# Stepping a state-space layer through the forget-gate attention, with score corrections over 128 rows and neighbourhood keys by column

## The chip, the cores and the metric

The kernel runs on 1 core of one Trainium2 chip. The metric is the device time of the whole program in microseconds; the time before is the median of 3 runs.

## The reference

The input is one sequence of 512 tokens (an 8 x 64 grid) with 1024 features. Two layers of a first block are followed by one layer of a second block, all in float32.

```python
# first block, twice: three branches, gated and merged
y_a = neighbourhood_attention(na_q, na_k, na_v, na_rpb)  # 8 heads of 64; 8 rows x 16 columns of keys
y_b = gqa_attention(q, k, gq_v)                          # 8 query heads, 2 key heads
y_c = spatial_gating(sg_u, sg_v, ...)
merged = sum(sigmoid(gate_r) * ((y_r * silu(z_r)) @ w_br_r) for r in "abc")
h = layer_norm(ALPHA * x + merged @ w_out + b_out)
...
# second block: forget-gate attention, a chunked state-space mixer, a diagonal state-space layer
s = q @ k.T / 8 + cum[q] - cum[k]                        # causal, cum = cumsum(log_sigmoid(f))
y_fox = softmax(s) @ v                                   # 8 heads of 64
y_ssd = ssd_mixer(z, xbc, dt_raw, ...)                   # conv, chunks of 128, 8 heads
y_s5 = glu(gelu(state_space(u)))                         # 32 groups of 16, complex state of 64
merged = sum(sigmoid(gate_r) * (y_r @ w_branch_r) for r in range(3))
x = layer_norm_2(ALPHA * x + merged @ w_out)
x = layer_norm_2(ALPHA * x + conv_ffn(x))
```

## The kernel before

Every product with weights keeps float32 accuracy by splitting each operand into a rounded high part and a low rest (`load_w`, L76 and L78, for weights) and adding three matmuls: high by high, low by high, high by low (`mm3`, L99 to L101). Low parts of weights are made on GpSimd or VectorE; `self.lo_gp` is a pattern of 0 (VectorE) and 1 (GpSimd) that is gone through load by load. Weight loads, and all other transfers, are issued on SP's queue.

Projections are *jobs*: one of 512 columns by 128 features is 24 matmuls in four portions of six. Jobs stand in `self.queue`; `fill(n)` runs n portions, so that the attention loops can put them between their own steps. The kernel is written with a tile framework: at build time a planner fixes the order of each engine's instructions from its own estimates of durations, with the written order as the priority, and adds the waits. So an instruction can stand before one that was written ahead of it, and a real duration that differs from the planner's shows up as a wait.

**Scores.** `heads_q` makes, for each head of a pair, a tile that holds the scaled query's high part on the head's 64 partitions and its low part on the other 64. `heads_k` makes a tile with the key's high part on both halves (L326, L327), and one tile `lo` for both heads, with each head's low part on that head's own 64 partitions (L328). A score is a matmul over 128 rows (q high and low against k high) and a correction over the head's 64 rows (q high against k low): L659 and L662 in `na`, L941 and L942 in `fox`. In `fox` a mask matmul in bf16 follows (L943).

**`na`** (neighbourhood attention, once in each layer of the first block) has 16 steps, four pairs of heads by four blocks of 16 columns. Keys lie in token order (row by row of the grid), so that a block's 256 keys are 8 pieces of 32; values are fetched from DRAM in the same order (L628), and the bias table goes with it (L634, L647).

**Second block.** `fox` queues its projections in a list `js` and then runs 34 iterations over 32 scores (8 heads by 4 query tiles); each calls `fill(1)` and `step(1)` twice. `ssd` does the same 16 times for `step`. `s5` is a generator that goes through the diagonal state-space layer in four groups F = 0 to 3: two matmul sets into two PSUM banks (L1408), rotations on VectorE and GpSimd (L1411 to L1417), two scans (L1422), rotations back (L1425 to L1431), the output matmuls (L1438, L1440), a GELU, a round trip through DRAM, and `close` (L1393, L1394). `step(n)` adds n to a counter and advances `s5` by one `yield` for each whole unit: `RF` per call in `fox`, `RS` in `ssd`, `RM` per portion in the first two merges. With `RF = 0.0` `s5` starts in `ssd`; a group needs the input `ub[F]`, which the job `uj(F)` projects and which passes through DRAM (`s5_in`, L1355 to L1360). PSUM has 3 banks for jobs ("mm"), 2 for scores ("s"), 2 for transposes ("t"), 1 for values ("v"); `s5` uses "mm" until the end of `ssd`, then "s" and "t".

Of the kernel before, what the change touches and what calls it, by code (L numbers as in the profile page):

```python
# [19 lines left out]
P = 128  # L20
# [5 lines left out]
class Net:  # L26
# [292 lines left out]

    def heads_k(self, src):  # L320

        nc, out, lo = self.nc, [], self.b2(F32R)
        for s in range(2):
            r, o = slice(64 * s, 64 * s + 64), slice(64 - 64 * s, 128 - 64 * s)
            k = self.b2(F32R)
            nc.scalar.copy(k[r], src[r])  # L326
            nc.scalar.copy(k[o], src[r])  # L327
            nc.vector.tensor_tensor(lo[r], src[r], k[r].bitcast(F32), op=ALU.subtract)  # L328
            out.append(k)
        return out, lo  # L330

    def z_gate(self, bias_name, bi, out):

# [256 lines left out]
    def na(self, l, vd):  # L590
# [12 lines left out]
        def kj(hp):  # L603
            def use(ps):
                kf = self.tmp()
                nc.scalar.activation(kf, ps, AF.Identity, bias=self.col(f"b{l}", 4 + hp))
                kzs[hp] = self.heads_k(kf)
            return self.fm_job(fm[4 + hp], use)

# [12 lines left out]

        def load(hp):
            vw = [self.b2(shape=(P, 4, P)) for _ in range(2)]
            vr = vd.rearrange("(r c) f -> r c f", c=64)
            for j in range(4):
                for half in range(2):
                    nc.sync.dma_start(vw[j // 2][:, 2 * (j % 2) + half], vr[4 * half:4 * half + 4, LO[j]:LO[j] + 32, hp * P:hp * P + P])  # L628
            vws[hp] = vw
            bts[hp] = []  # L630
            for s in range(2):
                t = self.ld(shape=(P, 8, 48))
                nc.sync.dma_start(t, a[f"rpb{l}"][2 * hp + s])
                bts[hp].append(t)  # L634

        def bias(i):

            if i == len(steps):
                return
            hp, j = steps[i]  # L640
            if j == 2:
                bms[i] = bms[i - 1]
                return
            bms[i] = self.b2(shape=(P, 2, 8, 32))
            x0 = (16, 8, 8, 0)[j]
            for s in range(2):
                nc.gpsimd.tensor_tensor(bms[i][:, s], bts[hp][s][:, :, x0:x0 + 32],  # L647
                                        self.namask[:, (0, 1, 1, 2)[j], None].to_broadcast([P, 8, 32]), op=ALU.add)

        def weights(hp, j):  # L650
            bm = bms[4 * hp + j]
            e = self.b2(shape=(P, 2, 256))
            mx, nmx, sm, rc = self.small(2), self.small(2), self.small(2), self.small(2)
            jq = slice(j * P, j * P + P)
            q, (ks, kl) = [x[:, jq] for x in qs[hp]], kzs[hp]
            ks, (kl,) = ([x.rearrange("p (r c) -> p r c", c=64)[:, :, LO[j]:LO[j] + 32] for x in xs] for xs in (ks, (kl,)))
            pss = [self.psum("s", (P, 256)) for _ in range(2)]
            for s in range(2):
                nc.tensor.matmul(pss[s], q[s], ks[s], start=True, stop=False)  # L659
            for s in range(2):  # L660
                r = slice(64 * s, 64 * s + 64)
                nc.tensor.matmul(pss[s], q[s][r], kl[r], start=False, stop=True)  # L662
            for s in range(2):
                nc.vector.tensor_tensor_reduce(out=e[:, s], in0=pss[s], in1=bm[:, s].rearrange("p r c -> p (r c)"), op0=ALU.add, op1=ALU.max,
                                               scale=1.0, scalar=-3e38, accum_out=mx[:, s:s + 1])
            nc.vector.tensor_scalar(nmx, mx, -1.0, None, op0=ALU.mult)
            for s in range(2):
                nc.scalar.activation(e[:, s], e[:, s], AF.Exp, bias=nmx[:, s:s + 1], accum_out=sm[:, s:s + 1])
            nc.vector.reciprocal(rc, sm)
            for s in range(2):  # L670
                nc.vector.tensor_scalar(e[:, s], e[:, s], rc[:, s:s + 1], None, op0=ALU.mult)
            return e
# [201 lines left out]
    def fox(self, xb, zz, step):  # L874
# [14 lines left out]
        def qj(hp):  # L889
            def use(ps):  # L890
                q[hp] = self.heads_q(ps, 0.125)
            return self.fm_job(fm[hp], use)
# [12 lines left out]
                xb[i] = z  # L905
            return self.fm_job(fm[12 + i], use)
        js = [self.tm_job([a[f"w2tm{c}"][0, 0], a[f"w2tm{c}"][0, 1]], vv(c)) for c in (1, 0)] + [qj(0), kj(0)]
        js += [xj(0), xj(1), qj(1), kj(1), xj(2), xj(3), qj(2), kj(2), xj(4), qj(3), kj(3), xj(5)]
        def zj(i):
            def use(ps):  # L910
                z = zz[i] = self.b2()
# [1 line left out]
                nc.scalar.activation(t, ps, AF.Tanh, scale=0.5)  # L913
                nc.vector.scalar_tensor_tensor(z, t, 1.0, ps, op0=ALU.add, op1=ALU.mult)
            return self.fm_job(fm[8 + i], use)
        js += [zj(i) for i in range(4)]

        def uj(F):
            return self.fm_job(fm[18 + F], lambda ps: self.s5_in(F, ps))
        self.ub = {}  # L920
        js += [uj(F) for F in range(4)]
        self.queue.append(self.jobs(js))
        self.fill(12)
        self.fdt(fd)
        self.lo_gp = (1, 1, 1, 0)
        self.fill(8)
        steps = [(hp, t, s) for hp in range(4) for t in range(4) for s in range(2)]
        sc, pes, cks, ys, po = {}, {}, {}, [], None
# [1 line left out]
        def weights(hp, t, s):  # L930
            h, n = 2 * hp + s, (t + 1) * P
            nn = max(n, 256)
            if t == 0:
                pc = self.psum("s")
                self.bcast_row(pc, h)
                cks[h] = self.b2()
                nc.scalar.copy(cks[h], pc)
            ps = self.psum("s")
            r = slice(64 * s, 64 * s + 64)
            qt, (ks, kl) = q[hp][s][:, t * P:t * P + P], kz[hp]  # L940
            nc.tensor.matmul(ps[:, :nn], qt, ks[s][:, :nn], start=True, stop=False)  # L941
            nc.tensor.matmul(ps[:, :nn], qt[r], kl[r, :nn], start=False, stop=False)  # L942
            nc.tensor.matmul(ps[:, n - P:n], self.identb, self.causal, start=False, stop=True)  # L943

            e = self.b2()
            mx, nm, sm, r = (self.small(1) for _ in range(4))
            nc.vector.tensor_tensor_reduce(out=e[:, :n], in0=ps[:, :n], in1=cks[h][:, :n], op0=ALU.subtract, op1=ALU.max,
                                           scale=1.0, scalar=-3e38, accum_out=mx)
            cq = self.cc[:, t, h:h + 1]
            nc.vector.tensor_scalar(nm, mx, cq, -1.0, op0=ALU.add, op1=ALU.mult)  # L950
            nc.vector.tensor_tensor(nm, nm, cq, op=ALU.add)
            nc.scalar.activation(e[:, :n], e[:, :n], AF.Exp, bias=nm, accum_out=sm)
            nc.vector.reciprocal(r, sm)
            return e, r
# [408 lines left out]
    def s5(self, gys, tags):  # L1363
# [34 lines left out]
        for F in range(4):  # L1398
# [33 lines left out]
            if F < 3:  # L1432
                w, tb = load(F + 1)
            yield
            py = self.psum(tags[1])
            for i in range(4):
                q = slice(i * P, i * P + P)
# [41 lines left out]
    def block2(self):  # L1479
# [1 line left out]
        gys = []  # L1481
        tags = ["mm", "mm"]
        s5 = self.s5(gys, tags)
        due = [0.0]

        def step(n):
            due[0] += n
# [10 lines left out]
        ya = self.fox(xb, zz, lambda n: step(RF))  # L1498
        yb = self.ssd(xb, zz, lambda n: step(RS))
        tags[:] = "s", "t"  # L1500
        self.lo_gp = (1,)
        merge(0, ya, RM, first=True)
        merge(1, yb, RM)
        for _ in s5:
# [43 lines left out]
NR = 6  # L1548
PSB = {"mm": 3, "s": 2, "t": 2, "v": 1}

RF = 0.0
RS = 0.5
RM = 1.5
BT = 4
MAGIC = 12582912.0
PI = 3.1415925
# [62 lines left out]
def _rpb_index():  # L1619
    r, cc = np.arange(P) // 16, np.arange(P) % 16  # L1620
    kr, x = np.arange(8), np.arange(48)
    ro = kr[None, :, None] - r[:, None, None] + 7
    co = np.clip(x[None, None, :] - 16 - cc[:, None, None] + 15, 0, 30)
    return (ro * 31 + co).reshape(-1)


def prepare(i):
# [18 lines left out]
    for l in range(2):  # L1646
        w, b = i["w_in"][l], i["b_in"][l]
        fmc = [w[:, 0:1024], w[:, 1536:2048], w[:, 2816:3328][:, pairs], w[:, 3328:3840], w[:, 4352:4864], w[:, 4864:7936]]
        a[f"w1fm{l}"] = _fm(np.concatenate(fmc, 1))
        tmc = [w[:, 2560:2816], w[:, 2048:2560], w[:, 3840:4352], w[:, 1024:1536]]  # L1650
        a[f"w1tm{l}"] = _tm(np.concatenate(tmc, 1))
        addc(f"b{l}", b.reshape(62, P).T)
        addc(f"zb{l}", b[2816:3328][pairs].reshape(4, P).T)
        addc(f"gvb{l}", b[2688:2816].reshape(P, 1))
        addr(f"qkb{l}", b[2048:2688])
        addr(f"qng{l}", np.concatenate([i["q_norm_g"][l], i["k_norm_g"][l]]))
        addr(f"sg{l}", np.concatenate([b[3840:4352], i["sg_ln_g"][l], i["sg_ln_b"][l]]))
        addr(f"b_out{l}", i["b_out"][l])
        addr(f"lnp_g{l}", i["ln_post_g"][l])
        addr(f"lnp_b{l}", i["ln_post_b"][l])  # L1660
        a[f"sgw{l}"] = np.ascontiguousarray(i["sg_w"][l].transpose(2, 0, 1))
        a[f"sgb{l}"] = np.ascontiguousarray(i["sg_b"][l].reshape(4, 2, P).transpose(1, 0, 2))
        a[f"rpb{l}"] = np.ascontiguousarray(i["na_rpb"][l].reshape(8, 15 * 31)[:, idx]).reshape(8, P, 8, 48)
        a[f"wbr{l}"] = np.stack([_pair(x) for x in (i["w_br_a"][l], i["w_br_b"][l][pairs], i["w_br_c"][l])])
        a[f"wout{l}"] = _wide(i["w_out"][l])
    w = i["w_in_2"][0]
# [59 lines left out]
```

## Time and profile before

| | |
|---|---|
| median of 3 runs | 2041.87 us (2039.82 to 2045.49) |
| profiled execution | 2042.89 us, its span 2041.1 us |
| TensorE busy (page) | 1988.1 us, 97% |
| VectorE, ScalarE, GpSimd busy | 1236.0 us, 863.2 us, 509.8 us |
| mean granted TensorE clock | 0.991 |

The span is the stretch that the profile covers; the time of the same execution is 1.8 us longer. A busy TensorE is one that has a matmul under way by the profile; the clock is the share of full speed that the chip granted.

### The profile page before, as it was taken

How to read it: one execution, taken by the hardware profiler on the slowest of the kernel's cores; microseconds unless marked ns; L12 is line 12 of the kernel's file. 1: busy time of each engine (PE TensorE's matmuls, PEld its weight loads, DVE VectorE, ACT ScalarE, POOL GpSimd, SP SyncE). 2: the span in 40 equal slices, each digit the busy share in tenths (PEclk: the TensorE clock that was granted, in tenths of full speed). 3: DMA queues.
4: the chain of work that ended last, by engine and by line, in shares of the span. 5: the costliest groups of instructions: out<-in, count | busy, mean ns of one | idle time of the engine just before them, and what ended most of it. 6: DMA issues, size and time to landing. Idle time of an engine off the chain costs nothing. (4 is left out here: it accounts for less than half of the span.)

```text
span 2041.1 us, 29326 instructions
## 1 busy us (share of the span) xinstructions
PE 1988.1 (97%) x10594; PEld 1653.3 (81%) x10594; DVE 1236.0 (61%) x2406; ACT 863.2 (42%) x1738; POOL 509.8 (25%) x594
## 2 busy tenths in 40 slices
PE   7999999999999999999999999998899999999998
PEld 7898877788799988777878877877688888888888
DVE  7776655766477766567545644365425477635655
ACT  3445446433235554564332466542233334423431
POOL 3343321100633436323610222235440000000000
PEclk9999999999999999999999999999899999999999
DMA  6432223333352322334353412143433423333332
GB/s 207 153 106 67 80 89 105 109 93 122 117 167 89 105 75 78 124 109 140 107 159 115 140 63 62 62 131 105 138 98 108 130 83 100 102 93 99 98 86 70
DMA packets 140464, 218.54 MB, mean 107 GB/s; under 512 B 19232, under 2 KB 44576, under 8 KB 140320
## 3 DMA queue, kind: packets, MB, share of 16 engines
q1 hardware_dynamic: 140320, 216.68, 33.7%
q8 instruction: 83, 1.36, 0.3%
q14 instruction: 61, 0.50, 0.1%
HBM read 196.70 MB, written 19.92 MB: 106 GB/s over the span
## 5 line engine op out<-in xcount | busy, mean ns | idle before, releaser
L76 ACT CAST wh<-wr 128x512 fp32r<-128x512 f32 x605 | 362.1, 618 | 587.5 <-PE psmm L100 273.7
L99 PE MATMUL psmm<-xh,wh 128*128 128x512 f32 (+1 forms) x1504 | 604.3, 402 | 1.5 <-DVE b L373 1.4
L100 PE MATMUL psmm<-xl,wh 128*128 128x512 f32 (+1 forms) x1504 | 588.1, 391 | 0.3 <-DVE xl L262 0.3
L101 PE MATMUL psmm<-xh,wl 128*128 128x512 f32 (+1 forms) x1504 | 587.4, 391 | 0.2 <-DVE wl L78 0.2
L78 DVE TENSOR_TENSOR wl<-wr,wh 128x512 fp32r<-128x512 f32 x526 | 374.6, 723 | 348.9 <-ACT wh L76 341.4
L101 PEld LDWEIGHTS psmm<-xh,wl 128*128 128x128 f32 x1504 | 283.5, 189 | 61.6 <-DVE wl L78 1.8
L99 PEld LDWEIGHTS psmm<-xh,wh 128*128 128x128 f32 x1504 | 284.1, 189 | 60.8 <-issue 3.4
L100 PEld LDWEIGHTS psmm<-xl,wh 128*128 128x128 f32 x1504 | 284.4, 189 | 52.7 <-DVE xl L262 0.7
L247 POOL TENSOR_TENSOR sm<-sm,mhalf 128x1 f32<-128x1 f32 x20 | 18.9, 947 | 648.4 <-DVE sm L245 648.4
L78 POOL TENSOR_TENSOR wl<-wr,wh 128x512 fp32r<-128x512 f32 x79 | 109.7, 1401 | 229.2 <-ACT wh L76 228.7
L99 PE MATMUL psmm<-wh,xh 128*128 128x256 f32 (+1 forms) x512 | 148.3, 291 | 2.0 <-DVE b L373 1.3
L100 PE MATMUL psmm<-wl,xh 128*128 128x256 f32 (+1 forms) x512 | 147.1, 287 | 2.0 <-DVE wl L78 1.8
L101 PE MATMUL psmm<-wh,xl 128*128 128x256 f32 (+1 forms) x512 | 147.3, 288 | 0.4 <-DVE xl L262 0.4
L465 POOL TENSOR_SCALAR b<-b,sm 128x512 f32<-128x512 f32 x64 | 101.1, 1580 | 163.6 <-DVE sm L296 158.4
L99 PE MATMUL psmm<-b,wh 128*128 128x512 f32 x304 | 119.8, 394 | 0.0
L100 PE MATMUL psmm<-b,wh 128*128 128x512 f32 x304 | 118.6, 390 | 0.0
L101 PE MATMUL psmm<-b,wl 128*128 128x512 f32 x304 | 118.5, 390 | 0.0
L99 PEld LDWEIGHTS psmm<-wh,xh 128*128 128x128 f32 x512 | 99.4, 195 | 4.0 <-DVE b L373 1.7
L100 PEld LDWEIGHTS psmm<-wl,xh 128*128 128x128 f32 x512 | 99.5, 194 | 3.8 <-DVE wl L78 2.6
L101 PEld LDWEIGHTS psmm<-wh,xl 128*128 128x128 f32 x512 | 99.4, 194 | 0.9 <-DVE xl L262 0.9
L647 POOL TENSOR_TENSOR b<-ld,namask 128x256 f32<-128x256 f32 x48 | 42.7, 916 | 151.0 <-PE psv L699 57.3
L294 ACT ACTIVATE b<-pss,sm 128x512 f32<-128x512 f32 x64 | 44.1, 689 | 81.5 <-DVE sm L291 81.0
(393 smaller groups left out, 3304.3 us busy)
## 6 DMA issues: line engine op xcount, KB each, us to landing
wr<-in_w1fm SPq DMA_DIRECT2D x192, 256.0 KB
wr<-in_w2fm SPq DMA_DIRECT2D x92, 256.0 KB
wr<-in_wup SPq DMA_DIRECT2D x88, 256.0 KB
wr<-in_wbr SPq DMA_DIRECT2D x72, 256.0 KB
wr<-in_w1tm SPq DMA_DIRECT2D x56, 256.0 KB
wr<-in_wout SPq DMA_DIRECT2D x48, 256.0 KB
wr<-in_wdown SPq DMA_DIRECT2D x43, 256.0 KB
ld<-in_rows SPq DMA_DIRECT2D x32, 256.0 KB
```

The costliest lines, as they stand in the source:

```text
L76: nc.scalar.copy(hi[:, c], raw)
L78: eng.tensor_tensor(lo[:, c], raw, hi[:, c].bitcast(F32), op=ALU.subtract)
L99: mm(ps, wh, xh, start=(first and k == 0), stop=False)
L100: mm(ps, wh, xl, start=False, stop=False)
L101: mm(ps, wl, xh, start=False, stop=(last and k == n - 1))
L247: nc.gpsimd.tensor_tensor(rs, ve, self.mhalf[:, :1], op=ALU.pow)
L294: nc.scalar.activation(e[:, :n], src, AF.Exp, bias=nm, scale=scale, accum_out=sm)
L465: nc.gpsimd.tensor_scalar(e, e, r, None, op0=ALU.mult)
L647: nc.gpsimd.tensor_tensor(bms[i][:, s], bts[hp][s][:, :, x0:x0 + 32], self.namask[:, (0, 1, 1, 2)[j], None].to_broadcast([P, 8, 32]), op=A ...
```

## The change

`heads_k` makes a tile `lo` for each head and copies the key's low part to the other 64 partitions too, so that the correction becomes a matmul over 128 rows. In `na` keys, values, bias table and mask are ordered column by column, which makes a block's keys one piece of 256. In `fox` the list of jobs is reordered: `uj` comes early, and most of `xj` late. `s5` gets one more `yield` ahead of the output matmuls, its counter starts at -7, `RF` becomes 0.5 and `RM` 0.5. The pattern of `lo_gp` becomes (0, 1) from `fox` to the end of the second merge.

```diff
     def heads_k(self, src):
-        nc, out, lo = self.nc, [], self.b2(F32R)
+        nc, out = self.nc, []
         for s in range(2):
...
-            k = self.b2(F32R)
+            k, lo = self.b2(F32R), self.b2(F32R)
             nc.scalar.copy(k[r], src[r])
             nc.scalar.copy(k[o], src[r])
             nc.vector.tensor_tensor(lo[r], src[r], k[r].bitcast(F32), op=ALU.subtract)
-            out.append(k)
-        return out, lo
+            nc.scalar.copy(lo[o], lo[r].bitcast(F32))
+            out.append((k, lo))
+        return out
...
-                nc.scalar.activation(kf, ps, AF.Identity, bias=self.col(f"b{l}", 4 + hp))
+                nc.scalar.activation(kf.rearrange("p (c r) -> p r c", r=8), ps.rearrange("p (r c) -> p r c", r=8),
+                                     AF.Identity, bias=self.col(f"b{l}", 4 + hp))
...
-            vr = vd.rearrange("(r c) f -> r c f", c=64)
+            vr = vd.rearrange("(r c) f -> c r f", c=64)
...
-                    nc.sync.dma_start(vw[j // 2][:, 2 * (j % 2) + half], vr[4 * half:4 * half + 4, LO[j]:LO[j] + 32, hp * P:hp * P + P])
+                    c0 = LO[j] + 16 * half
+                    nc.sync.dma_start(vw[j // 2][:, 2 * (j % 2) + half], vr[c0:c0 + 16, :, hp * P:hp * P + P])
...
             for s in range(2):
-                nc.tensor.matmul(pss[s], q[s], ks[s], start=True, stop=False)
-            for s in range(2):
-                r = slice(64 * s, 64 * s + 64)
-                nc.tensor.matmul(pss[s], q[s][r], kl[r], start=False, stop=True)
+                for i, k in enumerate(kzs[hp][s]):
+                    nc.tensor.matmul(pss[s], qs[hp][s][:, jq], k[:, jk], start=(i == 0), stop=(i == 1))
...
-        js += [xj(0), xj(1), qj(1), kj(1), xj(2), xj(3), qj(2), kj(2), xj(4), qj(3), kj(3), xj(5)]
...
-        js += [zj(i) for i in range(4)]
...
-        js += [uj(F) for F in range(4)]
+        js += [xj(0), qj(1), kj(1), uj(0), uj(1), qj(2), kj(2), xj(1), uj(2), qj(3), kj(3), uj(3), xj(2), xj(3), xj(4), xj(5)]
+        js += [zj(i) for i in range(4)]
...
-        self.lo_gp = (1, 1, 1, 0)
+        self.lo_gp = (0, 1)
...
-            nc.tensor.matmul(ps[:, :nn], qt, ks[s][:, :nn], start=True, stop=False)
-            nc.tensor.matmul(ps[:, :nn], qt[r], kl[r, :nn], start=False, stop=False)
+            nc.tensor.matmul(ps[:, :nn], qt, kh[:, :nn], start=True, stop=False)
+            nc.tensor.matmul(ps[:, :nn], qt, kl[:, :nn], start=False, stop=False)
...
             yield
+            yield
             py = self.psum(tags[1])
...
-        due = [0.0]
+        due = [-7.0]
...
-        self.lo_gp = (1,)
         merge(0, ya, RM, first=True)
...
-RF = 0.0
+RF = 0.5
 RS = 0.5
-RM = 1.5
+RM = 0.5
```

The bias table `rpb` and the mask are laid out to match (48 columns by 8 rows in place of 8 by 48).

## Rows read from the trace of the kernel before

**Rows 1.** The page's first part: busy time, share of the span, instructions.

```profile
PE 1988.1 (97%) x10594; PEld 1653.3 (81%) x10594; DVE 1236.0 (61%) x2406; ACT 863.2 (42%) x1738; POOL 509.8 (25%) x594
```

**Rows 2.** Windows of fox, ssd and the two merges: busy us (instructions), granted clock, DMA.

```profile
1172.40:1335.00 162.60, 161.50 (x837) 125.69 (x836) 72.70 (x220) 96.98 (x234) 39.30 (x31) 1.00 0.21 67
1335.00:1380.00 45.00, 44.60 (x293) 33.16 (x293) 29.42 (x44) 20.45 (x52) 15.51 (x16) 1.00 0.39 123
1380.00:1470.00 90.00, 72.58 (x364) 61.48 (x363) 48.29 (x56) 21.56 (x38) 47.63 (x36) 0.89 0.37 119
```

**Rows 3.** Waits from 1380 to 1470 us: total us, times, longest.

```profile
PE pst L1440 <- POOL b L1427: 15.7, 3, 6.2
```

**Rows 4.** Timeline of PE in the merges: start, duration, instruction, idle before.

```profile
1402.98 0.79 PE L1440 MATMUL pst<-b,ld 128*128 128x127 f32 x2 [4.70 <-POOL b L1427]
...
1404.00 0.63 PE L101 MATMUL psmm<-xh,wl 128*128 128x512 f32 x1
1404.43 0.63 PE L99 MATMUL psmm<-xh,wh 128*128 128x512 f32 x1
...
1409.18 1.95 PE L1408 MATMUL pss<-b,b 128*128 128x128 f32 x16
...
1432.47 0.79 PE L1440 MATMUL pst<-b,ld 128*128 128x127 f32 x2 [6.22 <-POOL b L1427]
...
1436.30 0.39 PE L1438 MATMUL pst<-b,ld 128*128 128x128 f32 x2
...
1459.58 0.49 PE L1440 MATMUL pst<-b,ld 128*128 128x127 f32 x2 [4.76 <-POOL b L1427]
...
1466.78 0.49 PE L101 MATMUL psmm<-xh,wl 128*128 128x512 f32 x1
```

**Rows 5.** Timeline of POOL ahead of the second of these waits.

```profile
1425.21 4.33 POOL L78 TENSOR_TENSOR wl<-wr,wh 128x512 fp32r<-128x512 f32 x2
1430.78 1.64 POOL L1427 TENSOR_TENSOR b<-b,b 128x512 f32<-128x512 f32 x1 [1.23 <-DVE b L1426]
```

**Rows 6.** Timeline of PE around one score of fox.

```profile
1221.56 0.36 PE L941 MATMUL pss<-b,b 128*128 128x256 f32 x1
1221.86 0.38 PE L942 MATMUL pss<-b,b 64*128 64x256 f32 x1
1222.17 0.23 PE L943 MATMUL pss<-causalb,identb 128*128 128x128 bf16 x1
1222.21 0.48 PE L99 MATMUL psmm<-xh,wh 128*128 128x512 f32 x1
1222.52 0.39 PE L100 MATMUL psmm<-xl,wh 128*128 128x512 f32 x1
1222.75 0.39 PE L101 MATMUL psmm<-xh,wl 128*128 128x512 f32 x1
```

**Rows 7.** Timeline of PE around two steps of na.

```profile
290.43 0.28 PE L659 MATMUL pss<-b,b 128*128 128x256 f32 x1
290.55 0.40 PE L101 MATMUL psmm<-xh,wl 128*128 128x512 f32 x1
...
346.81 0.50 PE L659 MATMUL pss<-b,b 128*128 128x256 f32 x2
347.25 0.39 PE L662 MATMUL pss<-b,b 64*128 64x256 f32 x2
347.56 0.50 PE L99 MATMUL psmm<-xh,wh 128*128 128x512 f32 x1
347.90 0.40 PE L100 MATMUL psmm<-xl,wh 128*128 128x512 f32 x1
```

**Rows 8.** The correction of na by its line: count, ns min/median/max, first and last start.

```profile
L662 PE MATMUL pss<-b,b x64: 381/383/386, 291.1 to 952.2; 64*128 64x256 f32 x64
```

**Rows 9.** The copy of a key's high part by its line, the same columns.

```profile
L327 ACT CAST b<-tmp x16: 617/619/622, 289.6 to 910.9; 64x512 fp32r<-64x512 f32 x16
```

**Rows 10.** Timeline of ACT: a copy that writes with a stride (s5_in).

```profile
1332.12 1.08 ACT L1355 COPY b<-psmm 128x512 f32<-128x512 f32 x1
```

More of the change, by code (lines that the diff above doesn't have):

```diff
@@ L631, in load @@
             for s in range(2):
-                t = self.ld(shape=(P, 8, 48))
+                t = self.ld(shape=(P, 48, 8))
                 nc.sync.dma_start(t, a[f"rpb{l}"][2 * hp + s])
@@ L643, in bias @@
                 return
-            bms[i] = self.b2(shape=(P, 2, 8, 32))
+            bms[i] = self.b2(shape=(P, 2, 32, 8))
             x0 = (16, 8, 8, 0)[j]
             for s in range(2):
-                nc.gpsimd.tensor_tensor(bms[i][:, s], bts[hp][s][:, :, x0:x0 + 32],
-                                        self.namask[:, (0, 1, 1, 2)[j], None].to_broadcast([P, 8, 32]), op=ALU.add)
+                nc.gpsimd.tensor_tensor(bms[i][:, s], bts[hp][s][:, x0:x0 + 32],
+                                        self.namask[:, (0, 1, 1, 2)[j], :, None].to_broadcast([P, 32, 8]), op=ALU.add)
         def weights(hp, j):
@@ L653, in weights @@
             mx, nmx, sm, rc = self.small(2), self.small(2), self.small(2), self.small(2)
-            jq = slice(j * P, j * P + P)
-            q, (ks, kl) = [x[:, jq] for x in qs[hp]], kzs[hp]
-            ks, (kl,) = ([x.rearrange("p (r c) -> p r c", c=64)[:, :, LO[j]:LO[j] + 32] for x in xs] for xs in (ks, (kl,)))
+            jq, jk = slice(j * P, j * P + P), slice(8 * LO[j], 8 * LO[j] + 256)
             pss = [self.psum("s", (P, 256)) for _ in range(2)]
             for s in range(2):
-                nc.tensor.matmul(pss[s], q[s], ks[s], start=True, stop=False)
+                for i, k in enumerate(kzs[hp][s]):
+                    nc.tensor.matmul(pss[s], qs[hp][s][:, jq], k[:, jk], start=(i == 0), stop=(i == 1))
             for s in range(2):
-                r = slice(64 * s, 64 * s + 64)
-                nc.tensor.matmul(pss[s], q[s][r], kl[r], start=False, stop=True)
-            for s in range(2):
-                nc.vector.tensor_tensor_reduce(out=e[:, s], in0=pss[s], in1=bm[:, s].rearrange("p r c -> p (r c)"), op0=ALU.add, op1=ALU.max,
+                nc.vector.tensor_tensor_reduce(out=e[:, s], in0=pss[s], in1=bm[:, s].rearrange("p c r -> p (c r)"), op0=ALU.add, op1=ALU.max,
                                                scale=1.0, scalar=-3e38, accum_out=mx[:, s:s + 1])
@@ L938, in weights @@
             ps = self.psum("s")
-            r = slice(64 * s, 64 * s + 64)
-            qt, (ks, kl) = q[hp][s][:, t * P:t * P + P], kz[hp]
-            nc.tensor.matmul(ps[:, :nn], qt, ks[s][:, :nn], start=True, stop=False)
-            nc.tensor.matmul(ps[:, :nn], qt[r], kl[r, :nn], start=False, stop=False)
+            qt, (kh, kl) = q[hp][s][:, t * P:t * P + P], kz[hp][s]
+            nc.tensor.matmul(ps[:, :nn], qt, kh[:, :nn], start=True, stop=False)
+            nc.tensor.matmul(ps[:, :nn], qt, kl[:, :nn], start=False, stop=False)
             nc.tensor.matmul(ps[:, n - P:n], self.identb, self.causal, start=False, stop=True)
@@ L1621, in _rpb_index @@
     kr, x = np.arange(8), np.arange(48)
-    ro = kr[None, :, None] - r[:, None, None] + 7
-    co = np.clip(x[None, None, :] - 16 - cc[:, None, None] + 15, 0, 30)
+    ro = kr[None, None, :] - r[:, None, None] + 7
+    co = np.clip(x[None, :, None] - 16 - cc[:, None, None] + 15, 0, 30)
     return (ro * 31 + co).reshape(-1)
@@ L1662, in prepare @@
         a[f"sgb{l}"] = np.ascontiguousarray(i["sg_b"][l].reshape(4, 2, P).transpose(1, 0, 2))
-        a[f"rpb{l}"] = np.ascontiguousarray(i["na_rpb"][l].reshape(8, 15 * 31)[:, idx]).reshape(8, P, 8, 48)
+        a[f"rpb{l}"] = np.ascontiguousarray(i["na_rpb"][l].reshape(8, 15 * 31)[:, idx]).reshape(8, P, 48, 8)
         a[f"wbr{l}"] = np.stack([_pair(x) for x in (i["w_br_a"][l], i["w_br_b"][l][pairs], i["w_br_c"][l])])
```

## The prediction

> **What bounds the kernel now.** I read the page first: TensorE is under way for 97% of the span, no other engine for more than 61% [rows 1]. So the time goes down only where TensorE is idle, or where its own instructions take less time. The windows by stage come next, because the change touches three stages. In the forget-gate attention TensorE works 161.5 of 162.6 us, at the full clock, while VectorE is busy for 72.7, ScalarE for 97.0 and GpSimd for 39.3 [rows 2]. In the state-space mixer it works 44.6 of 45.0 us. In the first two merges it works only 72.6 of 90.0 us, and the granted clock there is 0.89 [rows 2]. That stretch is the largest hole that the change can reach.
>
> The waits of the stretch name the cause: three waits of L1440, the output matmul of the layer `s5`, for a GpSimd instruction, L1427, 15.7 us together [rows 3]. The timeline shows them one by one, 4.70, 6.22 and 4.76 us, one for each of the groups 1 to 3 [rows 4]. It also shows what follows each: neighbouring matmuls of 512 columns start 0.43 us apart after the first wait [rows 4], where elsewhere they start 0.23 us apart [rows 6]; TensorE runs at the lower of its two levels, 1.2 in place of 2.4 GHz. The reason is seen on GpSimd: ahead of L1427 it makes the low parts of two weight tiles, 4.33 us [rows 5], and the planner has put L1440 where it expected the chain of VectorE and GpSimd to be done. With `RM = 1.5` a group gets only some six portions of projection as cover, about 6 x 6 x 0.23 = 8 us, for a chain that takes longer.
>
> **Part 1: `s5` is stepped in `fox`.** The schedule follows from the code. `fox` calls `step` 68 times at 0.5, so the counter gives 34 - 7 = 27 advances, the first at call 16, then one per iteration of 162.6 / 34 = 4.8 us. A group now has nine yields (eight for group 0, one more for the first load). So groups 0 to 2 are done when `fox` ends; `ssd` gives 16 x 0.5 = 8 advances, and group 3 ends at the start of the first merge. From a group's first matmuls to its output matmuls lie six advances, some 29 us of other TensorE work, in place of some 8.
>
> What it removes: the three waits and their neighbours in the merges. The waits are 15.7 us [rows 3]. The stretches at half speed run from 1402.98 to 1409.18, 1432.47 to 1436.30 and 1459.58 to 1466.78 [rows 4]. That is 6.2 + 3.8 + 7.2 = 17.2 us for work of half the time, so 8.6 us are given back. TensorE is idle for 90.0 - 72.6 = 17.4 us in the stretch [rows 2]; of the 1.7 us beyond the three waits I count 0.7 for the layer, a choice. Together 25.0 us. As a check, a mean clock of 0.89 over 90 us lacks 9.9 us at full speed, idle time included [rows 2].
>
> What it adds in `fox`: the matmuls of three groups, which leave the merges or `ssd` at the same price, so nothing in the sum. The elementwise work is bounded by all that the merges do now: 72.7 + 48.3 = 121 us of VectorE, 97.0 + 21.6 = 119 of ScalarE and 39.3 + 47.6 = 87 of GpSimd, all under 162.6 [rows 2]. No engine becomes the bound by its busy time. The transfers of the layer (its inputs through DRAM, its tables, its output) now stand on SP's queue among `fox`'s weight loads, and a transfer that waits holds those behind it; the jobs load two ahead, so a weight is late only after some 9 us. The same transfers go by in `ssd` today with TensorE idle for 0.4 of 45 us [rows 2].
>
> What I can't read off is how late single instructions come: the softmax of each score on VectorE and ScalarE, the two of three "mm" banks that a group holds until its rotations have read them, and group 0, whose input is projected only one iteration before its use. The lower bound is the `ssd` stretch, where group 0 runs today: 0.4 us, so some 1 us for three groups. The upper bound is that all 25 us come back. The schedule in `ssd` is the nearest to the new one, so I stay close to the lower end but allow one short wait per group with some lost clock: 5 us.
>
> **Part 2: corrections over 128 rows.** Around a score of `fox` the 128-row matmul takes 0.30 us to the next start and the 64-row one 0.31 [rows 6]. A 128-row matmul of 256 columns in front of another 128-row one takes 0.12 [rows 7]. Of the first 0.30, about 0.08 is the late weight load behind a very short matmul, as after the mask: 0.31 in place of 0.23 [rows 6]. That stays. So 0.61 - 0.24 - 0.08 = 0.29 us is the price of going to 64 rows and back, and 32 scores give 9.3 us.
>
> In `na` two high matmuls take 0.44, the two corrections 0.31, and the next projection matmul 0.34 in place of 0.23 [rows 6, 7]. Four at 0.12 with 0.10 for the entry behind the value matmuls (which keep their own shape) and 0.23 behind them make 0.81 in place of 1.09, so 0.28 us a step. There are 64 corrections, two a step [rows 8]: 32 steps, 9.0 us. TensorE is the bound in both places, so this goes through whole. The lower bound is a loss, since a second correction that now costs nothing beside the first will cost 0.12: -4 us. The upper is 0.40 a step, where the planner has split the pair and pays two switches: 13 us.
>
> A page speaks against this part. The Trainium skill, TensorE: Matmul & The Clock Gate, section "Why this matters for your kernels", advises the opposite for a contraction under 128 rows: put the operands on distinct row groups, so that the matmuls run together. The trace agrees in that the pair of corrections takes 0.31 us, as one does alone in `fox` [rows 6, 7]. By that rule alone `na` would lose 32 x 0.12 = 4 us and `fox` would gain nothing. The rows put the price of the changeover above it, and the sum goes by the rows.
>
> **Part 3: the rest, at nothing.** The copy of the low part is 24 more of some 0.62 us [rows 9], 15 us of a ScalarE that works 863 of 2041 us [rows 1]. The strided write of the keys costs at most the 1.08 us of the nearest one [rows 10], 8 times. Queued behind both are the casts of the next weights, which have two jobs' time; where a stage starts and its first scores wait for the key, the cover is gone and each costs about 1.2 us, three times, which the 5 us above must hold. Values and bias in column order move as many bytes in as many pieces of 512 bytes. `lo_gp` moves a quarter of the low parts in `fox`, and half of them in the merges, from GpSimd to VectorE, which has room [rows 2].
>
> **The sum.** 25.0 + 9.3 + 9.0 - 5 = 38.3 us. The profiled execution took 2042.9 us (its span and 1.8 around it), so 2004.6; the median of the runs is 1.0 lower, so the forecast is 2003.6 us.
>
> **The rivals.**
>
> *The waits move along (0.22).* The planner again puts matmuls of `s5` before their operands are there, now in `fox`. For: it misjudged L1427 three times. Against: 29 us of cover in place of 8, and fewer low parts on GpSimd. If 8 to 25 us are lost in place of 5, the time is 2007 to 2024; middle 2015.
>
> *The PSUM banks (0.06).* A group's two banks and a running job fill "mm", and the next job waits until one is read, some 6 us with 3 us of lost clock, in each of three groups: 28 us in place of 5, so 2027. Against: the `ssd` stretch, where group 0 holds the same banks.
>
> *The switch is not the price (0.06).* The 64-row matmuls run together and the 0.29 us has another cause, so that it stays. Then `fox` gains nothing, `na` loses 4, and the time is 2042 - 25 + 4 + 5 = 2026. It is what the rule of the Trainium skill named above would give. Against: the 0.30 and 0.31 show on both sides of the 64-row matmul alone.
>
> *Slower (0.03).* One mechanism: each of the 34 iterations waits for its own softmax, because the rotations and scans stand ahead of it on VectorE. It is slower from 43.3 / 34 = 1.3 us an iteration on; at 1.6 it would be 2042 - 43 + 54 = 2053. Against: VectorE is 45% busy in `fox` now and at most 75% after.
>
> *Nothing changes (0.02).* Half of the above at once; 2036 to 2048.
>
> **How the numbers follow.** My forecast, with its own range of 1994 to 2011, has 0.61; the lower end takes 13 us for `na` and 0 for new waits, the upper end 12 us of new waits. The range for 8 in 10 reaches into the moved waits: 1993 to 2022. A measurement of this kernel tells about 0.3% (6 us) from no change. Faster by more: 0.95; within it: 0.02; slower: 0.03.
>
> **What would show it.** In the merges L1440 and its waits are gone and the clock is 1.00; the stretch of 90 us shrinks by 25 us and by the matmuls that have moved. In `fox` L1440 and L1408 stand without waits, and all corrections read 128*128, 0.12 us apart for 256 columns. `na` is some 4.5 us shorter in each layer. The prediction is wrong if `fox` shows idle TensorE or a clock under 1.00 for more than a few us, or if a 128-row correction still takes 0.3 us.

## The result, and the profile after

| | before | after |
|---|---|---|
| median | 2041.8 us (2039.8 to 2045.5) | 2013.8 us (2012.2 to 2015.7) |
| ratio | 1 | 0.9861, 95% interval 0.9843 to 0.9879 |
| profiled execution | 2042.89 us | 2015.68 us (span 2013.9) |
| mean granted clock | 0.991 | 0.995 |

The kernel is 28 us faster. That is 10 us less than the sum of the prediction: its range holds the time, the likeliest case's own range of 1994 to 2011 doesn't, and the time lies in the middle of the rival "the waits move along" (2007 to 2024). Three readings show which terms came out. The busy line of the page answers to [rows 1]:

```profile
PE 1965.9 (98%) x10594; PEld 1645.1 (82%) x10594; DVE 1248.9 (62%) x2440; ACT 876.8 (44%) x1762; POOL 455.1 (23%) x560
```

TensorE executes as many matmuls as before and is under way for 22 us less. The windows of `fox`, `ssd` and the first two merges answer to [rows 2] (length; busy us of PE, PEld, DVE, ACT and POOL with their instructions; granted clock; DMA share and GB/s):

```profile
1176.00:1331.00 155.00, 147.64 (x849) 121.10 (x848) 96.99 (x237) 91.22 (x224) 38.43 (x34) 1.00 0.38 116
1331.00:1396.00 65.00, 59.97 (x386) 45.15 (x385) 42.52 (x67) 25.73 (x64) 19.04 (x18) 1.00 0.25 78
1396.00:1470.00 74.00, 73.54 (x328) 60.69 (x328) 23.51 (x34) 24.34 (x42) 18.39 (x14) 1.00 0.30 93
```

The merges are cured: 0.5 us idle in 74, at the full clock. But TensorE is now idle for 7.4 us in `fox` and for 5.0 in `ssd`, where it was 1.1 and 0.4. The waits of that stretch, 1157 to 1331 us, and under them, after the dots, those of `ssd` to 1396 (us in total, times, longest):

```profile
PE pst L304 <- ACT b L949: 5.6, 8, 1.3
PE pst L980 <- ACT yt L977: 1.7, 2, 1.3
PE pss L871 <- ACT b L935: 1.0, 1, 1.0
...
PE pss L1034 <- POOL b L1031: 2.0, 2, 1.3
PE pst L1119 <- POOL sm L1116: 1.2, 1, 1.2
PE pst L1079 <- DVE b L1071: 1.0, 2, 0.6
```

None is a wait of `s5` itself. The first of the eight waits of L304, 1.2 us, comes before `s5` has started, and a kernel that steps nothing through `fox` (e5 below) has it too. In `fox` they are waits of the attention: the transposes L304 of a score's weights wait for the exponential L949. What makes it late is seen around 1255 us, on VectorE, ScalarE and TensorE in turn:

```profile
1251.98 0.41 DVE L944 CUSTOM_DVE_ANT_0 b<-pss,b 128x256 f32<-128x256 f32 x1
...
1254.38 2.30 DVE L1419 TENSOR_TENSOR_SCAN b<-b,b 128x512 f32<-128x512 f32 x1 [1.98 <-POOL b L1413]
1256.60 0.18 DVE L947 TENSOR_SCALAR sm<-sm,cc 128x1 f32<-128x1 f32 x1
1256.70 1.21 DVE L1419 TENSOR_TENSOR_SCAN b<-b,b 128x512 f32<-128x512 f32 x1
1257.84 0.13 DVE L948 TENSOR_TENSOR sm<-sm,cc 128x1 f32<-128x1 f32 x1
```

```profile
1258.06 0.51 ACT L949 ACTIVATE b<-b,sm 128x256 f32<-128x256 f32 x1 [3.35 <-DVE sm L948]
```

```profile
1258.71 0.44 PE L304 MATMUL pst<-ident,b 128*128 128x128 f32 x2 [0.79 <-ACT b L949]
```

L944 has the maximum of the score at 1252.4. The two small operations on it, L947 and L948, take 0.3 us, but stand in VectorE's order behind the scans of `s5`: the first scan waits 1.98 us for GpSimd (L1413) and takes 2.30, and the second stands between the two. So the exponential starts 5.7 us after the maximum was there, with ScalarE idle for 3.35, and TensorE waits.

The scores themselves answer to [rows 6] and [rows 7] as forecast; first one of `fox`, then a step of `na` (start, duration, instruction):

```profile
1291.69 0.36 PE L938 MATMUL pss<-b,b 128*128 128x256 f32 x1
1291.89 0.28 PE L939 MATMUL pss<-b,b 128*128 128x256 f32 x1
1292.02 0.23 PE L940 MATMUL pss<-causalb,identb 128*128 128x128 bf16 x1
```

```profile
346.12 0.73 PE L661 MATMUL pss<-b,b 128*128 128x256 f32 x4
346.69 0.40 PE L99 MATMUL psmm<-xh,wh 128*128 128x512 f32 x1
346.92 0.40 PE L100 MATMUL psmm<-xl,wh 128*128 128x512 f32 x1
```

In `fox` the two take 0.20 + 0.13 = 0.33 us to the next start (0.61 before; 0.32 was forecast). In `na` the four take 0.57 and the matmul behind them 0.23: 0.80, where 0.81 was forecast and 1.09 stood before.

### The profile page after: what moved, and what is told of

Its sections match the earlier page's. It is cut to its first block, busy times and chain, and to the rows that moved or that the text cites. A ratio compares the mean times of both kernels' runs of the same rounds, so it can differ in the third digit from the quotient of the medians.

```text
span 2013.9 us, 29383 instructions
## 1 busy us (share of the span) xinstructions
PE 1965.9 (98%) x10594; PEld 1645.1 (82%) x10594; DVE 1248.9 (62%) x2440; ACT 876.8 (44%) x1762; POOL 455.1 (23%) x560
## 2 busy tenths in 40 slices
DMA packets 141233, 218.55 MB, mean 109 GB/s; under 512 B 20000, under 2 KB 45344, under 8 KB 141088
## 3 DMA queue, kind: packets, MB, share of 16 engines
q1 hardware_dynamic: 141088, 216.68, 34.8%
## 5 line engine op out<-in xcount | busy, mean ns | idle before, releaser
L78 DVE TENSOR_TENSOR wl<-wr,wh 128x512 fp32r<-128x512 f32 x560 | 398.8, 722 | 426.3 <-ACT wh L76 421.3
L99 PE MATMUL psmm<-xh,wh 128*128 128x512 f32 (+1 forms) x1504 | 598.0, 398 | 1.5 <-DVE b L374 1.4
L78 POOL TENSOR_TENSOR wl<-wr,wh 128x512 fp32r<-128x512 f32 x45 | 61.9, 1375 | 218.4 <-ACT wh L76 202.0
L650 POOL TENSOR_TENSOR b<-ld,namask 128x256 f32<-128x256 f32 x48 | 35.4, 764 | 153.8 <-PE pst L304 57.4
```

What stands on the lines that cost most here:

```text
L78: eng.tensor_tensor(lo[:, c], raw, hi[:, c].bitcast(F32), op=ALU.subtract)
L99: mm(ps, wh, xh, start=(first and k == 0), stop=False)
L650: nc.gpsimd.tensor_tensor(bms[i][:, s], bts[hp][s][:, x0:x0 + 32], self.namask[:, (0, 1, 1, 2)[j], :, None].to_broadcast([P, 32, 8]), op=A ...
```

## The experiments

Theory and rivals at the outset: the corrections are worth their 18 us, and the missing 10 us are waits that the stepping of `s5` makes in `fox` and `ssd`; or the corrections give less; or the extra copy of the key, the new list of jobs or the pattern of `lo_gp` costs it. A second question came with the first runs: what cured the merges, the place of `s5` or its pace there. Savings are worked out as (1 - ratio) x 2042 us. "The old schedule" is that of the kernel before: its list of jobs, `due` at 0, one `yield`, `RF = 0.0`, `RM = 1.5` and its `lo_gp`.

**Either part alone.** e1_scores is the kernel after with the old schedule; e2_steps is the kernel before with the new one.

```diff
# e1_scores, from the kernel after
-        js += [xj(0), qj(1), kj(1), uj(0), uj(1), qj(2), ...]
+        js += [xj(0), xj(1), qj(1), kj(1), xj(2), xj(3), ...]
...
-        self.lo_gp = (0, 1)
+        self.lo_gp = (1, 1, 1, 0)
...
-            yield
...
-        due = [-7.0]
+        due = [0.0]
...
+        self.lo_gp = (1,)
         merge(0, ya, RM, first=True)
...
-RF = 0.5
+RF = 0.0
-RM = 0.5
+RM = 1.5
```

> Part 2 alone: corrections over 128 rows and keys by column; the schedule of s5, the job list and lo_gp as before. My theory (going to 64 rows and back costs 0.29 us a score in fox and 0.28 us a step in na): 18 us less than before, about 2023.5 us; na shorter by some 4.5 us in each layer, and 128-row corrections 0.12 us to the next start for 256 columns. Rival (the changeover is not the price, the two 64-row corrections run side by side): no gain or up to 4 us more, 2042 to 2046 us.

> Part 1 alone: the schedule of s5 in fox with the job list, the further yield, the counter, RF, RM and lo_gp of the changed kernel; the scores as before. My theory as corrected by the changed kernel's trace (25 us of waits and lost clock gone from the merges, some 12 us of new short waits in fox and ssd): 13 us less than before, about 2029 us, and the short waits of the transposes L304 for the softmax still there. Rival (the new waits come from the longer making of the keys, one more copy on ScalarE): no new waits here, about 2017 us.

e1 took 2022.1 us, 0.9911 (0.9896 to 0.9925): 18.2 us, where the two terms were 18.3. From the first score of `na` to the last it is 103.3 us in each layer in place of 108.0: 9.4 us in the two, for a term of 9.0. In `fox`, from the third mask matmul to the first matmul of `ssd`, it is 134.3 us in place of 141.2: 6.8 us for 29 scores, 0.24 each, where 0.29 was forecast. The old waits of the merges are all there, the line of [rows 3] to the digit:

```profile
PE pst L1437 <- POOL b L1424: 15.7, 3, 6.2
```

e2 took 2028.2 us, 0.9938 (0.9923 to 0.9953): 12.7 us, where the prediction's steps say 25 - 5 = 20. Its transposes wait too, without the extra copy of a key's low part (one of the five waits, 0.9 us, stands in the kernel before as well):

```profile
PE pst L304 <- ACT b L951: 3.4, 5, 1.0
```

So the corrections are right in size, the copy isn't the cause, and the shortfall lies in the stepping. The two savings add up to 30.9; the change gave 28.4 (0.9861), inside the intervals.

**The pace alone.** e3_pace leaves `s5` where it was, in `ssd` and the merges, and gives a group more portions of projection there.

```diff
# from the kernel after; js as before
-        due = [-7.0]
+        due = [0.0]
...
-RF = 0.5
+RF = 0.0
-RM = 0.5
+RM = 0.32
```

> The changed kernel with s5 kept out of fox: RF 0.0, the counter from 0, RS 0.5, the old job list, and RM 0.32, so that a group in the merges has six advances of some three portions, about 25 us of cover. My theory (what the merges lacked was pace, and the new waits in fox and ssd come from s5's instructions on VectorE and ScalarE ahead of the softmax): the waits of the merges stay away and those of fox too, 10 to 12 us less than the changed kernel, about 2002 to 2004 us. Rival (only the place helps, the planner misjudges the chain in the merges at any pace): the waits of L1437 for GpSimd are back, with lost clock, 2024 us.

1996.6 us, 0.9785 (0.9769 to 0.9801): faster than both kernels. Windows of `fox`, `ssd` and the merges:

```profile
1172.00:1304.00 132.00, 131.81 (x730) 107.35 (x729) 67.94 (x201) 85.79 (x212) 19.93 (x16) 1.00 0.21 65
1304.00:1360.00 56.00, 55.46 (x368) 42.04 (x369) 37.25 (x59) 25.61 (x65) 17.17 (x17) 1.00 0.41 128
1360.00:1481.00 121.00, 121.00 (x600) 102.37 (x600) 75.51 (x86) 37.87 (x66) 52.71 (x39) 1.00 0.43 133
```

TensorE is idle for 0.7 us in 309, at the full clock. The merges need no help from `fox`.

**Which of the edits it was.** All from e3 but e5, which is the kernel after with `RF = 0.0`, `due = [0.0]` and `RM = 0.32` and so differs from e3 in the list of jobs alone; e6 has the old `lo_gp`, e7 the old pace, e11 one `yield`, e12 all low parts of that stretch on VectorE.

```diff
# e6_lo
-        self.lo_gp = (0, 1)
+        self.lo_gp = (1, 1, 1, 0)
...
+        self.lo_gp = (1,)
         merge(0, ya, RM, first=True)
# e7_fast
-RM = 0.32
+RM = 1.5
# e11_yield
-            yield
             yield
             py = self.psum(tags[1])
# e12_dve
-        self.lo_gp = (0, 1)
+        self.lo_gp = (0,)
```

> The third kernel (s5 kept out of fox, merges at RM 0.32, 1996.6 us) with the changed kernel's list of jobs: uj early, most of xj late. Theory A (the new waits of fox and ssd come from s5's own instructions): the list alone costs nothing, 1995 to 1999 us. Theory B (they come from xj's convolutions, which the new list piles up at the end of fox, and from ssd having its inputs late): most of the 17 us come back, 2006 to 2012 us, with waits of the transposes L304 for ScalarE.

> The third kernel with the low parts shared as before the change: three of four on GpSimd in fox and ssd, all on GpSimd in the first two merges. Theory A (pace alone cures the merges): 1995 to 2000 us. Theory B (fewer low parts on GpSimd, whose work ahead of the rotation delayed it, is what cures them): part of the three waits for GpSimd is back in the merges, 2005 us or more.

> The third kernel with RM back at 1.5, so that a group in the merges has some four portions of cover in place of some nineteen; the further yield and the new sharing of low parts stay. Theory A (pace): the three waits and the lower clock are back, 2015 to 2022 us. Theory B (the sharing of low parts and the further yield suffice): at most 4 us over the third kernel, 2000 us.

> The third kernel without the further yield ahead of the output matmuls, RM still 0.32: five advances of some three portions, about 21 us of cover. Theory A (the cover is long enough already): the same as with it, ratio 0.977 to 0.980. Theory B (the yield is what the chain needs): a wait of L1437 for GpSimd is back in each group, 0.983 or more.

> The third kernel with all low parts of weights on VectorE. Theory A (GpSimd's work slows VectorE's by holding it, so that moving more of it helps): the wait of fdt (L861) gets shorter than 2.7 us, and the whole 2 to 4 us faster, ratio about 0.977. Theory B (VectorE is busy for some 60% there and becomes late): waits of the softmax or of L1438 appear, ratio 0.980 or more.

| | median, us | ratio (95%) |
|---|---|---|
| e5_list | 1998.2 | 0.9784 (0.9769 to 0.9798) |
| e6_lo | 2003.0 | 0.9802 (0.9787 to 0.9817) |
| e7_fast | 2024.4 | 0.9913 (0.9897 to 0.9930) |
| e11_yield | 2000.6 | 0.9793 (0.9779 to 0.9808) |
| e12_dve | 1994.9 | 0.9767 (0.9748 to 0.9787) |

e5 equals e3: the list costs nothing that the whole time shows. e7 loses 0.0128 x 2042 = 26 us against e3, a little more than expected, and its waits and its clock are those of the kernel before; first its window from 1360 to 1450 us, then its wait:

```profile
1360.00:1450.00 90.00, 71.20 (x342) 59.65 (x342) 53.38 (x64) 21.39 (x36) 35.99 (x28) 0.91 0.38 119
```

```profile
PE pst L1438 <- POOL b L1424: 15.1, 3, 5.5
```

So the pace is the cause, and neither the extra `yield` nor `lo_gp` cures the merges at the old one. At the new pace e6, e11 and e12 overlap e3, so what these two edits are worth isn't settled. e12 is the fastest measured, but not clearly faster than e3. What moves with the pattern is one wait, for the VectorE chain of `fdt`, which prepares the forget gate ahead of `fox`; it is 2.7 us in e3, and here in e6 and in e12:

```profile
PE pst L861 <- DVE b L858: 3.6, 1, 3.6
```

```profile
PE pst L861 <- DVE b L858: 0.9, 1, 0.9
```

The clock moves the times too. In the profiles of e6 and e12 TensorE runs at its lower level for 10.2 us in `ssd`, which loses 5.1 us; in e3's profile it doesn't. In e12 the wait at its start is only 0.5 us, with narrow matmuls (L1112, L1119) around it; e3 has the same matmuls and the same wait. First the window, then the wait:

```profile
1353.70:1363.90 10.20, 10.15 (x37) 9.19 (x38) 4.07 (x7) 3.69 (x7) 2.31 (x3) 0.50 0.35 104
```

```profile
1353.75 2.08 PE L1119 MATMUL pst<-ident,sm 128*128 128x128 f32 x8 [0.47 <-POOL sm L1116]
```

**Where the waits of the stepping lie.** e8_late keeps the stepping through `fox` and takes `s5` out of `ssd`; e9_hop keeps all, and takes GpSimd out of the middle of the rotations.

```diff
# e8_late, from the kernel after
-RS = 0.5
-RM = 0.5
+RS = 0.0
+RM = 0.32
# e9_hop, from the kernel after
-            gp.tensor_tensor(t0, t0, t1, op=ALU.add)
-            gp.tensor_tensor(t2, t2, t3, op=ALU.subtract)
+            v.tensor_tensor(t0, t0, t1, op=ALU.add)
+            v.tensor_tensor(t2, t2, t3, op=ALU.subtract)
```

> The changed kernel with s5 at rest in ssd (RS 0.0) and at RM 0.32 in the merges, so that group 3 moves from ssd to the merges, while groups 0 to 2 stay in fox. Theory A (s5 in fox delays the softmax, s5 in ssd delays ssd): the waits of ssd go, some 5 us less than the changed kernel, about 2008 us; those of fox, some 8 us, stay. Theory B (ssd waits because its inputs are projected late by the new list, and group 3 has no part in it): no change, 2012 to 2015 us.

> The changed kernel with the two sums of the first rotation (L1413, L1414) on VectorE in place of GpSimd, so that a scan no longer stands at the head of VectorE's queue waiting for GpSimd, with the softmax's small operations behind it. Theory A (that wait at the head of the queue is what makes the softmax late): the waits of L304 for ScalarE fall by half or more, 3 to 6 us less than the changed kernel, ratio to the kernel before about 0.984. Theory B (VectorE simply has too much to do in fox, and now has 1.4 us more a group): the same or up to 4 us slower, 0.986 to 0.988.

e8 took 2011.1 us, 0.9845 (0.983 to 0.986). `fox` in e8, three groups stepped through it, and in e5, none, each from the same score to the first matmul of `ssd`:

```profile
1172.40:1326.69 154.29, 148.32 (x845) 121.60 (x844) 96.39 (x235) 90.65 (x221) 38.45 (x34) 0.99 0.36 117
```

```profile
1171.45:1302.51 131.06, 131.06 (x726) 106.44 (x724) 63.51 (x195) 85.89 (x211) 19.72 (x16) 1.00 0.25 81
```

The stage is 23.2 us longer. The 120 matmuls of three groups account for 13.3 us, by the time from each start to the next (some 0.11 each); 9.9 us are left. Of these 6.0 are idle time in the window. Some 1.6 are clock: behind one wait, eight matmuls of 512 columns start 0.41 to 0.43 us apart in place of 0.23.

```profile
1290.03 0.33 PE L304 MATMUL pst<-ident,b 128*128 128x128 f32 x1 [1.35 <-ACT b L949]
...
1291.10 0.63 PE L99 MATMUL psmm<-xh,wh 128*128 128x512 f32 x1
1291.52 0.63 PE L100 MATMUL psmm<-xl,wh 128*128 128x512 f32 x1
```

The other 2.3 stand as busy, and the runs don't say why. The whole kernel says nearly the same: from e5 to e8 it loses 0.0061 x 2042 = 12.5 us, and from e8 to the kernel after, which steps group 3 through `ssd`, 3.3 more (these two intervals overlap).

The expectation that the waits of `ssd` would go isn't met. With no `s5` in `ssd`, TensorE still waits there for 4.5 us:

```profile
PE pss L1034 <- POOL b L1031: 2.4, 3, 1.3
PE pst L1119 <- POOL sm L1116: 2.1, 2, 1.8
```

In e5, with the same list and one group in `ssd`, it waits for 2.5 us there, and in e3, with the old list, for 0.5. So group 3 isn't what makes `ssd` wait; the list has a part in it, and the rest is open.

e9 took 2011.4 us, 0.9847 (0.9832 to 0.9862). With the hop gone, the transposes still wait:

```profile
PE pst L304 <- ACT b L949: 4.7, 7, 1.2
```

That is 4.7 us in place of 5.6; the waits of L980 (1.7) are gone. Neither expectation is met, and the time overlaps that of the kernel after. `fox` alone says more: from the third mask matmul to the first matmul of `ssd` it takes 154.8 us in place of 157.4, with 4.9 us idle in place of 7.4. (In the whole this is blurred, since e9's granted clock is 0.80 from 1375 to 1400 us, in `ssd`, where that of the kernel after is 1.00.) All eight scans of e9 take 1.20 to 1.23 us. So the wait for GpSimd ahead of the scan, read above, and the longer scan make some 2.5 of the 9.9 us, not the larger part, though the test isn't clean: it gives VectorE the two additions as well.

**The corrections by themselves.** e4_rows_only is e1 with keys, values, bias and mask of `na` in token order, as before; e10_none is e1 without the corrections.

```diff
# e4_rows_only, from e1
-                    nc.tensor.matmul(pss[s], qs[hp][s][:, jq], k[:, jk], ...)
+                    nc.tensor.matmul(pss[s], qs[hp][s][:, jq], k.rearrange("p (r c) -> p r c", c=64)[:, :, LO[j]:LO[j] + 32], ...)
...
# e10_none, from e1
-                for i, k in enumerate(kzs[hp][s]):
-                    nc.tensor.matmul(pss[s], qs[hp][s][:, jq], k[:, jk], ...)
+                nc.tensor.matmul(pss[s], qs[hp][s][:, jq], kzs[hp][s][0][:, jk], start=True, stop=True)
...
-            nc.tensor.matmul(ps[:, :nn], qt, kl[:, :nn], start=False, stop=False)
```

> The first of these kernels without the order by column: corrections over 128 rows, but keys, values and bias in token order as before, so that a block's keys are 8 pieces of 32. My theory (the column order by itself is worth nothing, the shape of the correction is all): the same as with the column order within 3 us, about 2023.5 us. Rival (reading keys in 8 pieces slows the matmuls or the bias on GpSimd costs): more than 5 us slower than the first, 2029 us or more.

> The first kernel (128-row corrections, schedule as before) without any correction: the product with the key's low part is left out of the scores of na and fox, the tiles are still made. My theory (a 128-row correction costs its columns, 0.12 us for 256, 0.17 for 384, 0.23 for 512): 64 x 0.12 + 16 x 0.12 + 8 x 0.17 + 8 x 0.23 = 12.8 us less than with them, about 2010 us; so the 64-row ones of the kernel before cost 31 us, 0.33 us each. Rival (matmuls of 256 columns are covered by the loads of weights around them): under 6 us less, 2017 us or more.

e4 took 2023.0 us, 0.9912 (0.9897 to 0.9927), as e1: the order by column is worth nothing that these runs can tell, and the rows alone make the gain. e10 took 2011.7 us, 0.9851 (0.9834 to 0.9867), 12.3 us less than e1. So the 96 corrections cost 12.3 / 96 = 0.13 us each over 128 rows, and (1 - 0.9851) x 2042 / 96 = 0.32 us each over 64 rows.

## Why the prediction was right, and where it was off

*Right: the merges, 25.0 us.* The three waits and the lost clock are gone, and e7 against e3 puts 26 us on them. But the reason that part 1 gave, that stepping through `fox` makes the cover, is only one way to get it: with the other edits kept, the old place at `RM = 0.32` gives as much (e3). And the low parts on GpSimd ahead of L1427, in which the prediction saw the reason, aren't what L1427 waited for last: [rows 5] itself has GpSimd idle for 1.23 us between them and L1427, waiting for VectorE. In e7, with half of the low parts on VectorE, the same instruction (L1424 there) still comes late, behind VectorE:

```profile
1407.01 1.65 POOL L1424 TENSOR_TENSOR b<-b,b 128x512 f32<-128x512 f32 x1 [2.94 <-DVE b L1423]
```

*Right: the corrections, 9.3 + 9.0 us.* e1 measures 18.2, `na` a little over its term and `fox` a little under. The price of the changeover, read from the neighbours of one matmul, held, and so the rival "the switch is not the price" (2026) is refuted. It was what the rule of the Trainium skill (TensorE: Matmul & The Clock Gate, "Why this matters for your kernels") would have given; e1 and e10 show that for these matmuls, single ones or pairs among others over 128 rows, following it is the dearer way, though the two of a pair did run together (0.31 us, [rows 7]).

*Off: the 5 us for new waits.* The step that failed is "the schedule in `ssd` is the nearest to the new one, so I stay close to the lower end". Measured, from e5 to the kernel after, it is (0.9861 - 0.9784) x 2042 = 15.7. Of these 12.5 come with the stepping through `fox` (e5 to e8); the 3.3 behind them are inside the intervals. Put in place of the 5, the 15.7 make 2003.6 + 10.7 = 2014.3; the measured median is 2013.8. With nothing in that place the sum gives 1998.6, and e5, which steps none of `s5` through `fox`, measured 1998.2. The range for 8 in 10 holds the time only because it was drawn out to take in the rival of the moved waits. `ssd` was the wrong neighbour: it had one group, and not the chain of `fox`, in which TensorE needs a softmax's result from VectorE and ScalarE within an iteration of 4.8 us. The bound by busy time was true (VectorE 97 of 155 us) and said nothing of how late single instructions come.

*The rivals.* "The waits move along" was right in size, though not in its picture: the matmuls of `s5` in `fox` have their operands, and those of the attention wait. That is the mechanism of "slower", softmaxes behind the rotations and scans, at some 0.4 us for each of the 34 iterations (12.5 / 34) where 1.3 would have decided. "The PSUM banks": no wait for an "mm" bank stands among those of `fox`. I also feared lost clock behind the new waits: in the profile of the kernel after the clock of `fox` stayed at 1.00, in that of e8 it cost some 1.6 us.

*Part 3, at nothing:* e1, which has the copy of the low part, gave its 18.2 us whole; e4 shows no cost of the strided write, and e5 none of the list in the whole time. The pieces are not quite as many as before, 141088 packets after and 140320 before; e4, in token order, has 140320 too and shows no price of the others.

*Open:* that the softmax's small operations stand behind the scans is read from the trace; how much of the 9.9 us in `fox` comes from this order alone, and what the 2.3 us of longer busy time are, isn't settled. e9 suggests that the hop to GpSimd and the longer scan aren't most of it. Nor is it settled why `ssd` waits in e8 with no `s5` in it.

## What to carry to other kernels

When a background chain is late, try first how fast it is advanced at its old place: here one constant (1.5 to 0.32) brought all that the move brought, without the move's 16 us. Before work is put into a stage in which TensorE is never idle, look at that stage's shortest chain between engines and at what will stand ahead of its small instructions, since busy shares don't show it. And price a matmul by the starts of its neighbours: by e10 and e1 a 64-row correction cost 0.32 us, and a 128-row one, with twice the rows, 0.13.

## What the runs showed of the hardware

In the merges before, three gaps of 4.70 to 6.22 us were each followed by a stretch at the lower level. Short gaps went either way: in the kernel after the granted clock of `fox` stayed at 1.00 with 7.4 us of idle time in 155, its longest wait 1.35 us; in e8 the same wait at the same place, 1.35 us, was followed by a stretch at the lower level, and in e12 a wait of 0.47 us among narrow matmuls was, for 10.2 us. What decides between them isn't shown.

The same scan on VectorE, 128 x 512, took 2.30 us twice in the kernel after, both times with the addition L1414 begun on GpSimd shortly before it, and 1.20 to 1.23 the other six times. At one of those L1414 began shortly after the scan, and then took 2.14 itself in place of 1.29. In e9, which has these additions on VectorE, all eight scans took 1.20 to 1.23.

A second 64-row correction right behind the first was free (0.31 us for the pair [rows 7], 0.31 for one [rows 6]), yet all of them together cost 30.4 us, against 12.3 over 128 rows.
